# Inverse roots of the norms on GpSimd, and the modulations' products ranked behind 1500 later instructions

## The chip, the cores and the metric

One core of a Trainium2 chip runs the whole program in one launch. The metric is the device time of one execution in microseconds, the median of the runs shown. The engines are TensorE (PE; its weight loads are listed apart as PEld), VectorE (DVE), ScalarE (ACT), GpSimd (POOL) and SyncE (SP), which issues most of the DMAs.

## The reference

A model of 256 tokens with 1024 channels goes through two blocks of two layers each. The first block's layers mix a gated linear recurrence, an mLSTM and a memory attention, then apply a dense feed-forward (layer 0) or a mixture of eight experts (layer 1). The second block is modulated: a condition vector gives each norm a scale and a shift, and each residual a gate.

```python
def rms_norm(x, g):
    xf = x.astype(jnp.float32)
    y = xf * lax.rsqrt(jnp.mean(xf * xf, axis=-1, keepdims=True) + EPS)
    return (y * g.astype(jnp.float32)).astype(x.dtype)
...
def modulate(h, shift, scale):
    return h * (1 + scale) + shift
```

The six modulation vectors of a layer are the condition after a silu, times a 1024 x 6144 matrix, plus a bias. They depend on the conditions alone, so they can be computed at any time before the second block. There are two conditions, that of the tokens and that of a context stream; layer 1 uses the context's first two vectors only.

## The kernel before, in words

**Matmuls in three products.** Every float32 matmul is made of three products of rounded halves: a weight block of 1 MB comes in by a DMA on SP into one of three `raw` tiles (`load`), ACT rounds it to `hi` (L149), DVE subtracts to get `lo` (L150), and PE multiplies hi and lo with the split activations (`proj`, L171 and L175). DVE so has one 128x1024 subtraction to do for every block that PE uses.

**The order of the work.** The program is written as one sequence; a scheduler places each instruction on its engine by rank among those that are ready by its own reckoning, and the rank is the place in the program unless the code shifts it. The result is one fixed list for each engine. An engine runs its list in order: an instruction that has to wait holds up all behind it.

**The mixers.** `mixer` (called for layers 0 and 1 of the first block) first makes the memory attention's queries, scores and weights for four heads (`xa_a`, `xa_b`, `xa_c`). In the last round it adds `gate_rows`, a serial chain of some 20 small DVE steps on 4x256 rows (L399 to L409, a softplus and two scans), whose result PE transposes (L413), and `ml_a`, the first head of the mLSTM: a causal convolution of 8 DVE steps (L344, L347), a silu (L503 on ACT, L504 on DVE) and the split into halves (L368 on ACT, L369 on DVE), which PE needs as the operand of the block products (L171, into `ps_b`). The rest of the mixer is projections with `merge`, `ml_b`, `rg_a` and the like.

**The modulations.** `ada(n)` takes n of a layer's 48 slices. For each it loads 512 KB of the transposed matrix into one of two `adaw` tiles (L1157, on SP) and multiplies it on DVE with the silu of each condition, summing along the row (L1163, one instruction of 128x1024 for each condition with an accumulator). `ada` is called at fixed steps of the mixers (L720, L732, L759) and of the feed-forwards (L839), with the counts of the table `ADA`; `ada_end` does what is left, adds the bias and is followed by the gains. Layer 0's 96 products are made during the first block, layer 1's 64 during the first feed-forward of the second block. `issue_after` binds each product to come behind the last `lo` split that was written before it.

**The norms.** `squares` sums the squares (ACT and DVE, then PE with a column of ones, L251); `rms` scales the sums (L258); `rsqrt` computes an inverse root by a bit trick (L218) and two correction steps, 8 small DVE instructions, each on the result of the one ahead (L218 to L226); `spread` puts the two columns of the result on the diagonals of two 128x128 tiles (L235, DVE) and PE multiplies them with ones (L236), which spreads the roots over all partitions; then DVE multiplies the activations (L272). `rsqrt` is called 21 times: for the norms, and for the heads of the differential attention and of its context part, which do not use `spread`. `spread` runs 12 times, two diagonals each.

Of the kernel before, what the change touches and what calls it, by code (L numbers as in the profile page):

```python
# [8 lines left out]
F32 = mybir.dt.float32  # L9
# [4 lines left out]
OP = mybir.AluOpType  # L14
# [22 lines left out]


ADA = 1, 1, 3, 5


VECS = ["norm_mix_g", "conv_rg_w", "conv_rg_b", "rg_b_a", "rg_b_x", "rg_lambda", "conv_ml_w", "conv_ml_b",
# [67 lines left out]
class Kernel:  # L110
# [102 lines left out]
    def rsqrt(self, v, shape):  # L213


        nc = self.nc
        t = [self.work.tile([128, 8], F32, name=f"rq{i}", bufs=2)[0:shape[0], 0:shape[1]] for i in range(2)]
        nc.vector.tensor_scalar(t[0].bitcast(I32), v.bitcast(I32), -0.5, float(0x5f3759df), op0=OP.mult, op1=OP.add)  # L218
        nc.vector.tensor_mul(t[1], t[0], t[0])
        nc.vector.tensor_mul(t[1], t[1], v)  # L220
        nc.vector.scalar_tensor_tensor(t[1], t[1], -10.0 / 3, t[1], op0=OP.add, op1=OP.mult)

        nc.vector.scalar_tensor_tensor(t[0], t[1], 5.0, t[0], op0=OP.add, op1=OP.mult)
        nc.vector.tensor_mul(t[1], t[0], t[0])
        nc.vector.scalar_tensor_tensor(t[1], t[1], -0.5 * 0.375 ** 3, v, op0=OP.mult, op1=OP.mult)
        nc.vector.scalar_tensor_tensor(t[0], t[1], 1.5 * 0.375, t[0], op0=OP.add, op1=OP.mult)  # L226
        return t[0]

    def spread(self, cols):

        nc = self.nc
        ps = self.bank(self.small)
        for t in range(2):
            dg = self.work.tile([128, 128], F32, name="diag", bufs=2)
            nc.vector.tensor_scalar(dg, self.ident, cols[:, t:t + 1], None, op0=OP.mult)  # L235
            nc.tensor.matmul(ps[:, 0, t * 128:(t + 1) * 128], self.ones[:, :128], dg, start=True, stop=True)  # L236
        return ps

# [456 lines left out]
    def mixer(self, l, raw=None):  # L695
# [15 lines left out]
        for g in range(4):  # L711
# [6 lines left out]
            if g:  # L718
                self.xa_c(X, g - 1, yx)
            self.ada(ADA[2 * l])  # L720
        merged = self.big("merged")
# [3 lines left out]
        for g in range(4):  # L725
# [5 lines left out]
            self.ml_b(M, l, g)  # L731
            self.ada(ADA[2 * l])  # L732
            self.merge(G, l, 2, yx, merged, g)
# [18 lines left out]
        for g in range(4):  # L752
# [5 lines left out]
            if l == 0:  # L758
                self.ada(ADA[0])  # L759
        for j in range(4):  # L760
# [7 lines left out]
    def ffn(self, hs, w1, w3, w2, ff, add, ada=0, between=None, begun=None):  # L768
# [63 lines left out]
        for u in range(n):  # L832
            up(u)
            if u and (one or u < n - 1):
                down([u - 1])
            if begun and u == 0:
                begun()
            else:
                self.ada(ada)  # L839
# [309 lines left out]
    def ada(self, n=1):  # L1149

        nc = self.nc
        for _ in range(n):
            if not self.ada_left:
                break
            l, c = self.ada_left.pop(0)
            raw = self.adap.tile([128, D], F32, name="adaw", bufs=2)
            nc.sync.dma_start(raw, self.A["ada_t"][l, 128 * c:128 * c + 128])  # L1157
            with self.tc.issue_after(self.last_lo.ins):
                for name, s in self.silu.items():
                    if name == "c_ctx_2" and l == 1 and c >= 16:  # L1160
                        continue
                    pr = self.adap.tile([128, D], F32, name="prod", bufs=1)
                    nc.vector.scalar_tensor_tensor(pr, raw, 1.0, s, op0=OP.mult, op1=OP.mult,  # L1163
                                                   accum_out=self.mod[name, l][:, c:c + 1])
# [583 lines left out]
    def second(self):  # L1748
        tc, A = self.tc, self.A
        with ExitStack() as c1:  # L1750
# [8 lines left out]
            with tc.tile_pool(name="adap2", bufs=2) as self.adap:  # L1759
                self.ffn(hs, A["ffn_w1_2"][0], A["ffn_w3_2"][0], A["ffn_w2_2"][0], HID,  # L1760
                         lambda s, j, ps: self.add_mod(s, 0, 1, j, ps), ADA[3], between, lambda: self.ada_layer(1))
            with tc.tile_pool(name="att1", bufs=4) as self.att:
# [75 lines left out]
    def first(self):  # L1838
        tc, A = self.tc, self.A
        with ExitStack() as c1:  # L1840
# [5 lines left out]
            for l in range(2):  # L1846
                self.mixer(l, raw)
                if l == 0:
                    h = self.norm(self.x, self.vec("norm_ffn_g", 0), "h")
                    self.xa_kv(1, 0)  # L1850
                    self.ffn([h], A["ffn_w1"][0], A["ffn_w3"][0], A["ffn_w2"][0], D_FF, self.add_x, ADA[1])
            self.ada_end()
# [38 lines left out]
```

## Time and profile before

| | |
|---|---|
| median of 3 runs | 3192.14 us (3191.67 to 3192.84) |
| the profiled execution | 3190.43 us, its span 3188.6 us |
| mean granted TensorE clock | 0.983 of full speed |
| PE busy | 3094.2 us (97%) |
| DVE busy | 2480.8 us (78%), 3619 instructions |
| ACT busy | 1852.6 us (58%) |
| POOL busy | 70.1 us (2%), 102 instructions |
| HBM | 220 GB/s over the span |

Busy times are averages over stages with different limits: in the first block's mixers and the dense feed-forwards PE has hardly a gap, while in the expert layer (about 1200 to 2160 us) the transfers run at 340 to 350 GB/s and DVE is over 90% busy. A row of the timeline gives start and duration in us, engine, line, operation, tiles, and in brackets the idle time ahead of it with what ended it. "xN" folds N instructions in a row.

### The profile page before, as it was taken

How to read it: one execution, taken by the hardware profiler on the slowest of the kernel's cores; microseconds unless marked ns; L12 is line 12 of the kernel's file. 1: busy time of each engine (PE TensorE's matmuls, PEld its weight loads, DVE VectorE, ACT ScalarE, POOL GpSimd, SP SyncE). 2: the span in 40 equal slices, each digit the busy share in tenths (PEclk: the TensorE clock that was granted, in tenths of full speed). 3: DMA queues.
4: the chain of work that ended last, by engine and by line, in shares of the span. 5: the costliest groups of instructions: out<-in, count | busy, mean ns of one | idle time of the engine just before them, and what ended most of it. 6: DMA issues, size and time to landing. Idle time of an engine off the chain costs nothing. (4 is left out here: it accounts for less than half of the span.)

```text
span 3188.6 us, 53070 instructions
## 1 busy us (share of the span) xinstructions
PE 3094.2 (97%) x21140; PEld 2838.1 (89%) x21140; DVE 2480.8 (78%) x3619; ACT 1852.6 (58%) x2612; POOL 70.1 (2%) x102
## 2 busy tenths in 40 slices
PE   8999999999899999999999999999998999989999
PEld 8899999999899898888888888887988999987999
DVE  7668866678778669999999999997876876676555
ACT  5446644444458457887778878776654222256444
POOL 0000000000000000000000000000320000010000
PEclk9999999999999999999999999999998999999999
DMA  7354656555445559999999999997643444430353
GB/s 273 130 175 159 217 179 219 210 193 213 165 160 180 187 188 345 351 344 348 349 347 335 356 344 341 349 346 241 189 115 128 172 165 166 161 127 31 133 185 119
DMA packets 130873, 712.30 MB, mean 223 GB/s; under 512 B 23352, under 2 KB 35000, under 8 KB 53816
## 3 DMA queue, kind: packets, MB, share of 16 engines
q1 hardware_dynamic: 122552, 701.48, 61.0%
q0 software_dynamic: 8064, 7.34, 1.4%
q8 instruction: 167, 2.74, 0.3%
q14 instruction: 90, 0.74, 0.1%
HBM read 700.38 MB, written 1.05 MB: 220 GB/s over the span
## 5 line engine op out<-in xcount | busy, mean ns | idle before, releaser
L149 ACT CAST hi<-raw 128x1024 fp32r<-128x1024 f32 x1192 | 1233.5, 1051 | 829.7 <-PE ps_a L171 356.6
L150 DVE TENSOR_TENSOR lo<-raw,hi 128x1024 fp32r<-128x1024 f32 x1192 | 1426.5, 1221 | 352.2 <-ACT hi L149 340.0
L171 PE MATMUL ps_a<-hh,hi 128*128 128x256 f32 x2128 | 525.0, 283 | 0.2 <-DVE ks L1261 0.2
L171 PE MATMUL ps_a<-hl,hi 128*128 128x256 f32 x2128 | 524.4, 283 | 0.1
L171 PEld LDWEIGHTS ps_a<-hh,hi 128*128 128x128 f32 x2128 | 401.2, 189 | 4.1 <-issue 2.4
L171 PEld LDWEIGHTS ps_a<-hl,hi 128*128 128x128 f32 x2128 | 401.0, 188 | 3.9 <-issue 3.5
L974 PE MATMUL ps_a<-hi,xsh 128*128 128x512 f32 x896 | 355.0, 396 | 0.0
L975 PE MATMUL ps_a<-hi,xsl 128*128 128x512 f32 x896 | 353.9, 395 | 0.0
L976 PE MATMUL ps_a<-lo,xsh 128*128 128x512 f32 x896 | 351.7, 397 | 0.0
L175 PE MATMUL ps_a<-hh,lo 128*128 128x256 f32 x2128 | 299.3, 282 | 0.0
L175 PEld LDWEIGHTS ps_a<-hh,lo 128*128 128x128 f32 x2128 | 273.8, 188 | 0.5 <-issue 0.4
L825 PE MATMUL ps_b<-gh,lo 128*128 128x256 f32 x752 | 212.3, 283 | 0.0
L824 PE MATMUL ps_b<-gl,hi 128*128 128x256 f32 x752 | 212.1, 283 | 0.0
L823 PE MATMUL ps_b<-gh,hi 128*128 128x256 f32 x752 | 210.5, 283 | 0.0
L975 PEld LDWEIGHTS ps_a<-hi,xsl 128*128 128x128 f32 x896 | 168.3, 188 | 40.0
L976 PEld LDWEIGHTS ps_a<-lo,xsh 128*128 128x128 f32 x896 | 168.3, 188 | 39.5 <-DVE lo L150 0.6
L974 PEld LDWEIGHTS ps_a<-hi,xsh 128*128 128x128 f32 x896 | 168.4, 188 | 37.8 <-issue 0.4
L1006 PE MATMUL ps_b<-hi,mgl 128*128 128x512 f32 x448 | 175.3, 393 | 1.5 <-DVE mgl L992 1.5
L1005 PE MATMUL ps_b<-hi,mgh 128*128 128x512 f32 x448 | 173.8, 391 | 0.0
L825 PEld LDWEIGHTS ps_b<-gh,lo 128*128 128x128 f32 x752 | 144.0, 192 | 0.0
L824 PEld LDWEIGHTS ps_b<-gl,hi 128*128 128x128 f32 x752 | 144.0, 191 | 0.0
L1007 PE MATMUL ps_b<-lo,mgh 128*128 128x512 f32 x448 | 143.8, 396 | 0.0
(564 smaller groups left out, 5675.0 us busy)
## 6 DMA issues: line engine op xcount, KB each, us to landing
raw<-in_moe_w_dram SPq DMA_DIRECT2D x336, 1024.0 KB, 5.9
raw<-in_ffn_w_dram SPq DMA_DIRECT2D x108, 1024.0 KB, 4.8
raw<-in_w_in_dram SPq DMA_DIRECT2D x64, 1024.0 KB, 4.8
adaw<-in_ada_t_dram SPq DMA_DIRECT2D x96, 512.0 KB, 3.8
raw<-in_w_in_ab_dram SPq DMA_DIRECT2D x24, 1024.0 KB, 5.6
raw<-in_w_kv_dram SPq DMA_DIRECT2D x16, 1024.0 KB, 5.0
raw<-in_w_br_xa_dram SPq DMA_DIRECT2D x8, 1024.0 KB, 6.1
raw<-in_w_br_ml_dram SPq DMA_DIRECT2D x8, 1024.0 KB, 4.9
```

The costliest lines, as they stand in the source:

```text
L149: self.last_hi = nc.scalar.copy(hi, view)
L150: self.last_lo = nc.vector.tensor_sub(lo, view, hi.bitcast(F32))
L171: nc.tensor.matmul(out, wh[:, k, :], b[:, k, :], start=start and n == 0, stop=False, skip_group_check=skip)
L175: nc.tensor.matmul(out, wl[:, k, :], xh[:, k, :], start=False, stop=stop and k == nk - 1, skip_group_check=skip)
L823: nc.tensor.matmul(o, wh[:, 0, fs], gh[:, k, :], start=st, stop=False, skip_group_check=True)
L824: nc.tensor.matmul(o, wh[:, 0, fs], gl[:, k, :], start=False, stop=False, skip_group_check=True)
L825: nc.tensor.matmul(o, wl[:, 0, fs], gh[:, k, :], start=False, stop=end, skip_group_check=True)
L974: nc.tensor.matmul(o, xs[0][:, kk, :], wh[:, k, :], start=(kk == 0), stop=False)
L975: nc.tensor.matmul(o, xs[1][:, kk, :], wh[:, k, :], start=False, stop=False)
L976: nc.tensor.matmul(o, xs[0][:, kk, :], wl[:, k, :], start=False, stop=(kk == 7))
L1005: nc.tensor.matmul(o, g[0][:, kk, :], wh[:, 0, ns], start=(c + kk == 0), stop=False)
L1006: nc.tensor.matmul(o, g[1][:, kk, :], wh[:, 0, ns], start=False, stop=False)
```

## The change

All but the first instruction of `rsqrt` move from DVE to GpSimd; there the seven fused steps are written as ten, since each is a plain product or a product or sum with constants, and a third small tile holds one intermediate. The two diagonals of `spread` move to GpSimd as well. The products of `ada` are no longer bound behind the last `lo` split; instead their rank is lowered by 1500 instructions.

```diff
+LATER = 1500
...
     def rsqrt(self, v, shape):
         nc.vector.tensor_scalar(t[0].bitcast(I32), v.bitcast(I32), -0.5, float(0x5f3759df), op0=OP.mult, op1=OP.add)
-        nc.vector.tensor_mul(t[1], t[0], t[0])
-        nc.vector.tensor_mul(t[1], t[1], v)
-        nc.vector.scalar_tensor_tensor(t[1], t[1], -10.0 / 3, t[1], op0=OP.add, op1=OP.mult)
-
-        nc.vector.scalar_tensor_tensor(t[0], t[1], 5.0, t[0], op0=OP.add, op1=OP.mult)
-        nc.vector.tensor_mul(t[1], t[0], t[0])
-        nc.vector.scalar_tensor_tensor(t[1], t[1], -0.5 * 0.375 ** 3, v, op0=OP.mult, op1=OP.mult)
-        nc.vector.scalar_tensor_tensor(t[0], t[1], 1.5 * 0.375, t[0], op0=OP.add, op1=OP.mult)
-        return t[0]
+        pool, (y, w) = nc.gpsimd, t
+        pool.tensor_mul(w, y, y)
+        pool.tensor_mul(w, w, v)
+
+        u = self.work.tile([128, 8], F32, name="rq2", bufs=2)[0:shape[0], 0:shape[1]]
+        pool.tensor_scalar(u, w, -10.0 / 3, None, op0=OP.add)
+        pool.tensor_mul(u, u, w)
+        pool.tensor_scalar(u, u, 5.0, None, op0=OP.add)
+        pool.tensor_mul(y, y, u)
+        pool.tensor_mul(w, y, y)
+        pool.tensor_mul(w, w, v)
+        pool.tensor_scalar(w, w, -0.5 * 0.375 ** 3, 1.5 * 0.375, op0=OP.mult, op1=OP.add)
+        pool.tensor_mul(y, y, w)
+        return y
...
     def spread(self, cols):
-            nc.vector.tensor_scalar(dg, self.ident, cols[:, t:t + 1], None, op0=OP.mult)
+            nc.gpsimd.tensor_scalar(dg, self.ident, cols[:, t:t + 1], None, op0=OP.mult)
...
     def ada(self, n=1):
             nc.sync.dma_start(raw, self.A["ada_t"][l, 128 * c:128 * c + 128])
-            with self.tc.issue_after(self.last_lo.ins):
+
+            with self.tc.high_priority(offset=-LATER):
                 for name, s in self.silu.items():
```

The lists of the engines change with it. Line numbers of the changed kernel are higher: by 1 up to `rsqrt`, by 6 or 7 behind it (L369 is L375 there, L1163 is L1170, L1157 is L1163). Numbers behind a tile's name are those of its copies.

**DVE, mixer of layer 0, from the convolution of the first mLSTM head to its last half.** Before:

```order
L344 TENSOR_SCALAR cv<-pad,vecs 128x256 x2
L494 TENSOR_TENSOR y_xal<-ps_b,y_xah 128x512
L347 SCALAR_TENSOR_TENSOR cv<-pad,vecs,cv 128x256
L150 TENSOR_TENSOR lo<-raw,hi 128x1024
L347 SCALAR_TENSOR_TENSOR cv<-pad,vecs,cv 128x256 x2
L494 TENSOR_TENSOR y_xal<-ps_b,y_xah 128x512
L347 SCALAR_TENSOR_TENSOR cv<-pad,vecs,cv 128x256 x3
L504 SCALAR_TENSOR_TENSOR cv<-th,cv 128x512
L369 TENSOR_TENSOR half<-cv,half 128x512
L369 TENSOR_TENSOR half<-pad,half 128x512
```

With the change:

```order
L353 SCALAR_TENSOR_TENSOR cv<-pad,vecs,cv 128x256 x2
L1170 SCALAR_TENSOR_TENSOR prod,mod_c_570<-adaw,silu_c_574 128x1024
L353 SCALAR_TENSOR_TENSOR cv<-pad,vecs,cv 128x256 x2
L1170 SCALAR_TENSOR_TENSOR prod,mod_c_ctx_572<-adaw,silu_c_ctx_580 128x1024
L500 TENSOR_TENSOR y_xal<-ps_b,y_xah 128x512
L353 SCALAR_TENSOR_TENSOR cv<-pad,vecs,cv 128x256 x2
L1170 SCALAR_TENSOR_TENSOR prod,mod_c_570<-adaw,silu_c_574 128x1024
L510 SCALAR_TENSOR_TENSOR cv<-th,cv 128x512
L1170 SCALAR_TENSOR_TENSOR prod,mod_c_ctx_572<-adaw,silu_c_ctx_580 128x1024
L375 TENSOR_TENSOR half<-cv,half 128x512
L1170 SCALAR_TENSOR_TENSOR prod,mod_c_570<-adaw,silu_c_574 128x1024
L375 TENSOR_TENSOR half<-pad,half 128x512
```

Between these steps stood one `lo` split and no product; now there are five products in the same piece, one ahead of nearly every step. In the whole list up to and with the row of `half<-pad`, there are 10 products before and 61 with the change; the number of `lo` splits is the same. The last of layer 0's 96 products stands at the third `z` (L556 before) of this mixer; before, 16 were made by the end of the mixer's mLSTM part and the rest in the feed-forward and in the mixer of layer 1, where none is left now. Layer 1's 64 products begin at the second block's feed-forward in both.

**PE, the same place, from the attention of the last head to the first block product on `half`.** Before, with the projections (`hh`, `hl`) still between:

```order
L175 MATMUL ps_a<-hh,lo 128x256 x2
L490 MATMUL ps_b<-xpt,xv 128x256 x4
L484 MATMUL ps_b<-consts,xp 128x128 x4
L175 MATMUL ps_a<-hh,lo 128x256 x6
L190 MATMUL ps_a<-y_xah,hi 128x256
L191 MATMUL ps_a<-y_xal,hi 128x256
L490 MATMUL ps_b<-xpt,xv 128x256 x4
L192 MATMUL ps_a<-y_xah,lo 128x256
L171 MATMUL ps_b<-hi,half 128x256
L171 MATMUL ps_b<-lo,half 128x256
```

With the change:

```order
L176 MATMUL ps_a<-hh,lo 128x256 x8
L191 MATMUL ps_a<-y_xah,hi 128x256
L192 MATMUL ps_a<-y_xal,hi 128x256
L193 MATMUL ps_a<-y_xah,lo 128x256
L419 MATMUL ps_b<-consts,r_1188 128x4 x2
L469 MATMUL ps_b<-xk,xq 128x256 x4
L490 MATMUL ps_b<-consts,xp 128x128 x4
L496 MATMUL ps_b<-xpt,xv 128x256 x4
L490 MATMUL ps_b<-consts,xp 128x128 x4
L496 MATMUL ps_b<-xpt,xv 128x256 x4
L172 MATMUL ps_b<-hi,half 128x256
```

Before, the transposes of `gate_rows` (L413, not in this piece) stand well ahead of it and some 50 projections follow them; with the change these projections stand ahead of the transposes, and nothing but the attention is left between the transposes and `half`.

**DVE, the norm of the context stream ahead of the second block's feed-forward (from about 2404 us).** Before:

```order
L223 SCALAR_TENSOR_TENSOR rq_33911<-rq_33912,rq_33911 128x2
L1144 SCALAR_TENSOR_TENSOR silu_c_ctx_34529<-prod,silu_c_ctx_34529 128x1024
L150 TENSOR_TENSOR lo<-raw,hi 128x1024
L247 TENSOR_TENSOR sq<-sq 128x512
L224 TENSOR_TENSOR rq_33912<-rq_33911 128x2
L1223 SCALAR_TENSOR_TENSOR x<-ps_a,mod_c_562,x 128x256 x2
L150 TENSOR_TENSOR lo<-raw,hi 128x1024
L1145 TENSOR_SCALAR silu_c_ctx_34529<-silu_c_ctx_34529 128x1024
L225 SCALAR_TENSOR_TENSOR rq_33912<-rq_33912,ms 128x2
L226 SCALAR_TENSOR_TENSOR rq_33911<-rq_33912,rq_33911 128x2
L1684 TENSOR_SCALAR sinks<-sinks 128x16
L235 TENSOR_SCALAR diag<-consts,rq_33911 128x128 x2
```

With the change:

```order
L151 TENSOR_TENSOR lo<-raw,hi 128x1024
L219 TENSOR_SCALAR rq_33971<-ms 128x2
L151 TENSOR_TENSOR lo<-raw,hi 128x1024
L1150 SCALAR_TENSOR_TENSOR silu_c_34591<-prod,silu_c_34591 128x1024
L151 TENSOR_TENSOR lo<-raw,hi 128x1024
L253 TENSOR_TENSOR sq<-sq 128x512
L1151 TENSOR_SCALAR silu_c_34591<-silu_c_34591 128x1024
L1230 SCALAR_TENSOR_TENSOR x<-ps_a,mod_c_570,x 128x256 x2
L151 TENSOR_TENSOR lo<-raw,hi 128x1024 x2
L1150 SCALAR_TENSOR_TENSOR silu_c_ctx_34597<-prod,silu_c_ctx_34597 128x1024
L151 TENSOR_TENSOR lo<-raw,hi 128x1024
L278 TENSOR_TENSOR xg<-xg,ps_b 128x512 x4
```

The steps of `rsqrt` stood among `lo` splits and the silu of the conditions; only its first one (L219 in the changed kernel) is left in the list, and the product with the spread roots (L278) stands behind five of those splits and three silu steps, with neither roots nor diagonals between. On POOL each `rsqrt` is now a row of ten instructions and each `spread` a pair behind them. SP's list has 12 `adaw` loads in a row ahead of the `raw` load that follows the first mLSTM head's blocks, where one stood.

## Rows read from the trace of the kernel before

**Rows 1.** The page: busy time of the engines, and transfer rates in 40 equal slices.

```profile
PE 3094.2 (97%) x21140; PEld 2838.1 (89%) x21140; DVE 2480.8 (78%) x3619; ACT 1852.6 (58%) x2612; POOL 70.1 (2%) x102
...
GB/s 273 130 175 159 217 179 219 210 193 213 165 160 180 187 188 345 351 344 348 349 347 335 356 344 341 349 346 241 189 115 128 172 165 166 161 127 31 133 185 119
```

**Rows 2.** Windows: PE, PEld, DVE, ACT, POOL busy us (x instructions), PEclk, DMA share, GB/s.

```profile
25.80:151.54 125.74, 120.34 (x954) 116.46 (x954) 90.60 (x148) 58.69 (x95) 0.00 (x0) 0.99 0.50 181
140.00:160.00 20.00, 14.60 (x81) 13.36 (x81) 12.09 (x22) 9.37 (x15) 0.10 (x1) 0.83 0.25 80
160.00:280.00 120.00, 120.00 (x930) 112.07 (x929) 80.60 (x122) 59.89 (x88) 0.41 (x4) 1.00 0.47 163
2440.00:2800.00 360.00, 360.00 (x3019) 359.85 (x3018) 254.64 (x417) 93.94 (x115) 0.00 (x0) 1.00 0.45 159
```

**Rows 3.** Line L1163 and line L1157: the products, and their loads.

```profile
L1163 DVE SCALAR_TENSOR_TENSOR prod<-adaw,silu_c x96: 1210/1219/1228, 46.6 to 2775.9; 128x1024 f32<-128x1024 f32 x96
...
  DMA adaw<-in_ada_t_dram: 10.3, 12
```

```profile
DMA to landing us min/median/max: 3.3/3.8/12.3
```

**Rows 4.** DVE timeline, mixer of layer 0: head 3's scores to the last half.

```profile
134.68 0.69 DVE L467 TENSOR_REDUCE mx<-ps_b 128x2 f32<-128x512 f32 x1 [1.76 <-PE ps_b L463]
...
139.68 1.22 DVE L1163 SCALAR_TENSOR_TENSOR prod<-adaw,silu_c 128x1024 f32<-128x1024 f32 x1
...
140.94 1.22 DVE L1163 SCALAR_TENSOR_TENSOR prod<-adaw,silu_c_ctx 128x1024 f32<-128x1024 f32 x1
...
150.86 0.68 DVE L369 TENSOR_TENSOR half<-pad,half 128x512 fp32r<-128x512 f32 x1
```

**Rows 5.** PE timeline at the same place.

```profile
132.44 0.28 PE L413 MATMUL ps_b<-consts,r 4*128 4x4 f32 x2
...
150.79 0.58 PE L171 MATMUL ps_b<-hi,half 128*128 128x256 f32 x1 [5.40 <-ACT half L368]
151.17 0.42 PE L171 MATMUL ps_b<-lo,half 128*128 128x256 f32 x1
...
157.66 0.40 PE L175 MATMUL ps_b<-half,lo 128*128 128x256 f32 x2
```

**Rows 6.** The same place in the mixer of layer 1: DVE, then PE.

```profile
803.72 0.69 DVE L467 TENSOR_REDUCE mx<-ps_b 128x2 f32<-128x512 f32 x1 [1.76 <-PE ps_b L463]
...
822.43 0.68 DVE L369 TENSOR_TENSOR half<-pad,half 128x512 fp32r<-128x512 f32 x1
```

```profile
822.36 0.58 PE L171 MATMUL ps_b<-hi,half 128*128 128x256 f32 x1 [8.74 <-ACT half L368]
```

**Rows 7.** The context norm ahead of the second block's feed-forward: DVE, then PE.

```profile
2404.64 0.16 DVE L218 TENSOR_SCALAR rq<-ms 128x2 int32<-128x2 int32 x1
...
2418.31 0.16 DVE L226 SCALAR_TENSOR_TENSOR rq<-rq,rq 128x2 f32<-128x2 f32 x1
...
2419.79 0.48 DVE L235 TENSOR_SCALAR diag<-consts,rq 128x128 f32<-128x128 f32 x2
```

```profile
2420.22 0.77 PE L236 MATMUL ps_b<-diag,consts 128*128 128x128 f32 x2 [5.83 <-DVE diag L235]
```

**Rows 8.** Norms for which PE waits, DVE and PE: before the router, before the last feed-forward.

```profile
1098.73 0.16 DVE L218 TENSOR_SCALAR rq<-ms 128x2 int32<-128x2 int32 x1
...
1100.10 0.16 DVE L226 SCALAR_TENSOR_TENSOR rq<-rq,rq 128x2 f32<-128x2 f32 x1
1100.30 0.48 DVE L235 TENSOR_SCALAR diag<-consts,rq 128x128 f32<-128x128 f32 x2
```

```profile
2980.37 1.01 PE L236 MATMUL ps_b<-diag,consts 128*128 128x128 f32 x3 [2.14 <-DVE diag L235]
```

**Rows 9.** POOL by line and shape: busy us, mean ns.

```profile
L1238 POOL TENSOR_TENSOR rt<-rt,late 128x256 f32<-128x256 f32 x18 | 14.5, 803 | 72.7 <-PE ps_a L1236 70.0 <-DVE qc L1253 2.6
...
L1456 POOL TENSOR_TENSOR bias<-bias,late 128x1024 f32<-128x1024 f32 x4 | 9.5, 2373 | 0.3
...
L352 POOL MEMSET pad<- 128x6 f32 x16 | 1.6, 104 | 951.3 <-DVE half L369 781.8 <-DVE cv L347 169.2 <-POOLq L1886 0.3
```

**Rows 10.** The diagonals (L235) on DVE, and one beside POOL's work.

```profile
L235 DVE TENSOR_SCALAR diag<-consts,rq x20: 277/284/1904, 30.5 to 2980.2; 128x128 f32<-128x128 f32 x20
```

```profile
2233.36 1.90 DVE L235 TENSOR_SCALAR diag<-consts,rq 128x128 f32<-128x128 f32 x1
```

```profile
2232.79 2.39 POOL L1456 TENSOR_TENSOR bias<-bias,late 128x1024 f32<-128x1024 f32 x1
```

**Rows 11.** The memory's norm at the start: its diagonals on DVE, their matmuls on PE.

```profile
18.16 0.48 DVE L235 TENSOR_SCALAR diag<-consts,mem_r 128x128 f32<-128x128 f32 x2
```

```profile
21.59 0.61 PE L236 MATMUL ps_b<-diag,consts 128*128 128x128 f32 x4
```

## The prediction, made before the changed kernel ran

> **What bounds the kernel now.** I read the busy times first: PE is busy 97% of the span, DVE 78%, POOL 2% [rows 1]. So the time can fall only where PE waits (3188.6 - 3094.2 = 94 us in all), and it grows wherever PE has to wait longer. Next I read windows of the stages in which the products lie. From 160 to 280 us and from 2440 to 2800 us PE has no gap at all [rows 2]; there DVE work may come and go at no gain, as long as DVE keeps ahead. Then I looked for PE's gaps whose releaser is a DVE or ACT result: 5.40 us ahead of the first block product on `half` in the mixer of layer 0 [rows 5], 8.74 us at the same place of layer 1 [rows 6], 5.83 us ahead of the context norm's spreading [rows 7], and 2 to 4 us at norms with little beside them, such as 2.14 us before the last feed-forward [rows 8]. These four kinds of places are what the change touches.
>
> **The products in the mixer of layer 0.** One product occupies DVE for 1.22 us; two behind each other start 1.26 us apart, and the next instruction follows 1.15 us after [rows 4]; I take 1.15. Nothing makes a product urgent, but the new rank lets it go whenever the scheduler saw DVE free, and a fixed list keeps it there when the chip is late. The list of the changed kernel has 61 products up to the last `half` of the first head, 10 before: 51 more, or 51 x 1.15 = 58.7 us. Seven root steps of 0.16 us and a pair of diagonals of 0.48 us leave DVE in the same piece (durations as in [rows 8]): -1.6 us. From 25.8 us, when the conditions' silu is made, to 151.54 us, the end of that `half` (150.86 + 0.68, [rows 4]), DVE was busy 90.60 of 125.74 us, so idle for 35.1 us [rows 2]. If the products filled every idle moment, `half` would still end 58.7 - 1.6 - 35.1 = **22 us** later, at 173.5 us. That is the low end.
>
> Not every idle moment can be filled. The products need their loads: a pair uses its tile for 2.3 us, the next load lands 3.8 us after its issue [rows 3], and with two tiles a pair can come each (2.3 + 3.8) / 2 = 3.05 us. In the last stretch, from the gate rows on, 15 pairs stand with only short steps between them, which is about 2.7 us a pair by my estimate (2.3 us and two or three steps of 0.16 us); 0.35 us x 15 is some 5 us, of which I take 4. If half of the idle time stayed unfilled, `half` would come 22 + 17.5 = 40 us later: the high end. SP also puts 12 of these loads in a row ahead of a weight block, which then waits for the products that free the tiles. The added traffic itself fits: 26 more loads of 0.52 MB in 125.74 us are 108 GB/s on 181 [rows 2], below the 340 to 350 GB/s that other slices reach [rows 1].
>
> PE cannot hide this. In the changed list the projections that stood between the transposes of the gate rows and `half` lie ahead, so PE does them early, and behind the transposes (132.44 us before, [rows 5]) it has only the attention's few matmuls. It waits for the serial DVE chain, in which a product now stands ahead of almost every step. Afterwards PE is full to 280 us [rows 2], so what is lost is not regained. The half clock after the gap is no new cost: in 140 to 160 us the granted clock averaged 0.83 [rows 2], and the matmuls from 151.17 us on ran about 0.21 us apart until 157 us [rows 5]; a longer gap has the same end. Of the products left after `half` there are 35 instead of 6; 29 x 1.15 = 33 us fit in the 39.4 us that DVE idles in 160 to 280 us [rows 2], and PE is later too. I put **+26 us** (20 to 40) for this stage.
>
> **The mixer of layer 1 and the feed-forward** lose 80 products. In full stretches that is worth nothing. At the gap of 8.74 us, scores to last `half` took 822.43 + 0.68 - 803.72 = 19.4 us with six products between, in layer 0 150.86 + 0.68 - 134.68 = 16.9 us with two [rows 4, 6]: 0.63 us a product. Six gone give **-4 us** (0 to -8.7, the whole gap).
>
> **The context norm at 2404 us.** DVE takes 13.8 us from the first root step to the last, because splits stand between them, and PE waits 5.83 us [rows 7]. On POOL the steps stand alone (below, about 4 us with the diagonals), so the diagonals are done before PE asks. But the token stream's update now stands behind the norm's products in DVE's list, and PE then waits for the split activations. I take **-4 us** (0 to -10).
>
> **The price of a root on POOL.** No POOL instruction in the trace has a 128x2 shape. A memset of 128x6 takes 0.10 us, a two-input product of 128x256 takes 0.80 us, one of 128x1024 2.37 us [rows 9]. The line through the last two, (2.37 - 0.80) / 768 = 2.05 ns an element, leaves 0.28 us at no elements; I take that, step for step. Ten steps are 2.8 us (1.0 by the memset, 8.0 by the 128x256 product), against 1.53 us on DVE undisturbed (1098.73 to 1100.26, [rows 8]); the diagonals of 128 elements are 0.28 + 0.26 = 0.54 us each against 0.28 us. An exposed norm so becomes 1.4 us longer by the roots and 0.5 us by the diagonals. Three are fully exposed (before the router, before the last feed-forward, at the end), +5.7 us; four in the differential attention, the router's own root and the entry to the second block are partly so, and I take +2.3 us for them together. Sum **+8 us** (-2 by the low price, +30 by the high one). Norms with full PE work beside them cost nothing; the cover is the projections of the stage before.
>
> Here a rule speaks against the change. What the trace shows first: the memory's diagonals start at 18.16 us and their matmuls at 21.59 us [rows 11], so this first root has 2.9 us to spare and I cost it at nothing. The Trainium skill, page GPSIMD Engine Reference, section Instruction dispatch, says that the first call of freshly loaded code costs about 6 us that no row of a profile shows; by that rule the first root on POOL would overrun its slack by some 3 us and the sum below would be 3 us higher. No row of this trace shows it.
>
> **The sum.** 26 - 4 - 4 + 8 = +26 us on the profiled execution's 3190.4 us is 3216 us; the runs' median lies 1.7 us above that execution, so **3218 us**, 0.8% slower.
>
> **Rivals.**
> *The idle time swallows the products (faster).* In layer 1 an added product cost 0.63 us of the chain, not 1.15, since the chain waits for ACT and PE anyway. If that holds for the 51 of layer 0, they need 32 us, less than the 35.1 us of idle time, and `half` is not later. It decides at 35.1 / 51 = 0.69 us a product. Then nothing is lost there, and -6 in layer 1, -6 at the context norm and +2 at the norms give -10 us: 3182 us. For it: DVE idles 28% of that stretch. Against it: the layer 1 figure comes from six products in a chain full of waits, while in layer 0 some 30 of the 51 stand among splits, ahead of the gate rows, where DVE waits for little but ACT.
> *The gains and losses cancel.* A third of the 26 us stays (+9), layer 1 gives -6, the norm -6, the roots +3: 3192 us. It needs the same as the rival above, half true.
> *POOL is dear.* Each small step costs what the 128x256 product does, 0.8 us, and DVE is held meanwhile. For it: a diagonal that DVE began at 2233.36 us, while POOL worked from 2232.79 us on a bias tile, took 1.90 us where the median is 0.284 us [rows 10]. Then the norms cost +30 to +50 instead of +8, and the time is about 3255 us. Against it: the steps move two elements a partition, and the slow diagonal stood beside an instruction of 1024. The Trainium skill, page Advanced Engine Details and Errata, section VectorE Performance Modes, says that the second SBUF port of VectorE is shared with GpSimd and that the two block each other; the slow diagonal agrees (1.90 us against 0.284 us), and the rule would lengthen DVE work beside each root.
>
> **How the numbers follow.** The forecast gets 0.72, POOL dear 0.08, cancelling 0.10, faster 0.10. The forecast's own range is 3204 to 3240 (mixer 20 to 40, norms 0 to 12, the gaps -2 to -14). Down to the cancelling case and a little below it, 3190, and up to 3242, about 0.8 is held. A difference of 0.2%, 6.4 us, is about what can be told from no change: faster 0.10, same 0.10, slower 0.80.
>
> **What would show it.** In the mixer of layer 0, PE's gap ahead of the first block product on `half` grows from 5.4 us to 25 us or more, split between the gate rows' transposes, the scores and `half`, and that `half` ends at 173 us or later; no product lies in layer 1's chain and its gap is 4 to 5 us; the context norm's gap is below 2 us; ten POOL steps take about 2.8 us; the gap before the last feed-forward is about 4 us. I am wrong if `half` of layer 0 ends before 160 us, if POOL's steps take over 0.5 us each, or if PE gets new gaps between 160 and 280 us for late `lo` splits.

## The result, and the profile after

The changed kernel takes 3215.52 us (median of 4 runs, 3213.01 to 3217.53) against 3191.9 us for the kernel before beside it: a ratio of 1.0074 [1.0057, 1.0092], so 0.74% slower. The forecast was 3218 us. The total is right, and not all of its terms are: the products of layer 1, the roots with their norms and the mixer of layer 0 cost more than forecast, and a gain of about 18 us that the forecast did not know of paid for them.

The profiled execution took 3217.53 us (span 3215.8 us, mean granted TensorE clock 0.977). The busy line of its page answers to [rows 1]: DVE lost 27 us of work to POOL, which gained 102 us, and PE's busy time fell by 6 us while the span grew by 27.

```profile
PE 3088.1 (96%) x21140; PEld 2828.6 (88%) x21140; DVE 2454.0 (76%) x3448; ACT 1852.6 (58%) x2612; POOL 172.4 (5%) x336
```

**Mixer of layer 0.** Windows of the changed kernel (columns as in [rows 2]), the first of them from the silu of the conditions to the end of the first head's last `half`:

```profile
25.80:181.97 156.17, 126.78 (x957) 120.71 (x956) 144.10 (x242) 58.55 (x95) 9.06 (x12) 0.91 0.65 228
...
140.00:160.00 20.00, 7.27 (x31) 5.57 (x29) 18.52 (x36) 1.47 (x2) 0.00 (x0) 0.66 0.48 167
160.00:180.00 20.00, 6.26 (x21) 4.76 (x22) 18.97 (x39) 6.78 (x16) 0.00 (x0) 0.74 0.43 146
```

DVE is now busy 18.5 to 19.0 of 20 us around the gate rows and the attention, where it was busy 12.1 of 20 [rows 2], and PE only 6 to 7. The timeline of PE shows what it waited for, in the order of the serial chain (answers to [rows 5]):

```profile
145.16 0.39 PE L193 MATMUL ps_a<-y_xah,lo 128*128 128x256 f32 x1 [2.85 <-DVE lo L151]
...
154.90 0.37 PE L419 MATMUL ps_b<-consts,r 4*128 4x4 f32 x2 [9.36 <-DVE r L411]
...
162.96 3.58 PE L496 MATMUL ps_b<-xpt,xv 128*128 128x256 f32 x8 [3.28 <-ACT xpt L492]
...
179.75 0.58 PE L172 MATMUL ps_b<-hi,half 128*128 128x256 f32 x1 [10.06 <-ACT half L374]
```

On DVE one product stands ahead of each of the last two splits (answers to [rows 4]); the last one ends at 181.28 + 0.69 = 181.97 us, 30.4 us later than before:

```profile
178.39 1.22 DVE L1170 SCALAR_TENSOR_TENSOR prod<-adaw,silu_c_ctx 128x1024 f32<-128x1024 f32 x1
...
179.54 0.69 DVE L375 TENSOR_TENSOR half<-cv,half 128x512 fp32r<-128x512 f32 x1
180.14 1.23 DVE L1170 SCALAR_TENSOR_TENSOR prod<-adaw,silu_c 128x1024 f32<-128x1024 f32 x1
...
181.28 0.69 DVE L375 TENSOR_TENSOR half<-pad,half 128x512 fp32r<-128x512 f32 x1
```

**Mixer of layer 1.** Without products the gap of 8.74 us [rows 6] is 4.97 us:

```profile
837.25 0.58 PE L172 MATMUL ps_b<-hi,half 128*128 128x256 f32 x1 [4.97 <-ACT half L374]
```

**Norms.** A root on POOL where DVE does nothing beside it, ahead of the last feed-forward (POOL's timeline; the first and the last of ten steps, then the diagonals), and PE behind it, answering to [rows 8]:

```profile
3004.71 0.20 POOL L221 TENSOR_TENSOR rq<-rq 128x2 f32<-128x2 f32 x1 [60.57 <-DVE rq L219]
...
3007.28 0.20 POOL L232 TENSOR_TENSOR rq<-rq,rq 128x2 f32<-128x2 f32 x1
3007.57 1.19 POOL L241 TENSOR_SCALAR diag<-consts,rq 128x128 f32<-128x128 f32 x2
```

```profile
1114.95 1.38 PE L242 MATMUL ps_b<-diag,consts 128*128 128x128 f32 x4 [5.67 <-POOL diag L241]
...
2430.06 0.79 PE L242 MATMUL ps_b<-diag,consts 128*128 128x128 f32 x2 [2.90 <-POOL diag L241]
...
3008.24 1.38 PE L242 MATMUL ps_b<-diag,consts 128*128 128x128 f32 x4 [4.01 <-POOL diag L241]
```

Ten steps take 2.85 us from 3004.71 to 3007.57 us, a step 0.20 us with a start each 0.28 us, a diagonal 0.60 us. The gap before the last feed-forward grew from 2.14 to 4.01 us, that of the context norm (2430.06 us) shrank from 5.83 [rows 7] to 2.90 us.

### The profile page after: what moved, and what is told of

Read it like the earlier page. It is cut to its first block, busy times and chain, and to the rows that moved or that the text cites. A ratio compares the mean times of both kernels' runs of the same rounds, so it can differ in the third digit from the quotient of the medians.

```text
span 3215.8 us, 53166 instructions
## 1 busy us (share of the span) xinstructions
PE 3088.1 (96%) x21140; PEld 2828.6 (88%) x21140; DVE 2454.0 (76%) x3448; ACT 1852.6 (58%) x2612; POOL 172.4 (5%) x336
## 5 line engine op out<-in xcount | busy, mean ns | idle before, releaser
L829 PEld LDWEIGHTS ps_b<-gh,hi 128*128 128x128 f32 x752 | 142.9, 191 | 1.0 <-DVE ctx L1230 1.0
```

The lines of the kernel that those rows point to most:

```text
L829: nc.tensor.matmul(o, wh[:, 0, fs], gh[:, k, :], start=st, stop=False, skip_group_check=True)
```

## The experiments

**The two kernels again.** For a second trace of each on one chip; nothing edited.

> The kernel before, unchanged, for a second profile. In the last feed-forward (3000 to 3170 us), where the change moves nothing, PE's matmuls of 128x256 started 119.95 ns apart in the first profile of before and 118.3 ns apart in that of the change. If that pace belongs to the single execution or the chip, this profile shows any value near 118 to 120 ns, most likely that of its neighbours in this job; if it belongs to the kernel, it shows 119.9 ns again. Time 3190 to 3193 us either way.

> The changed kernel, unchanged, for a second profile on the same chip as the others of this job. 3213 to 3218 us. Pace of the matmuls in the last feed-forward 118.3 ns if the pace belongs to the kernel, that of the kernel before on this chip if it belongs to the execution. PE's gap ahead of the first block product on half in layer 0 and the waits just ahead of it add to 25 us again.

Measured: 3187.66 and 3216.74 us. Places agree: the block product on `half` starts at 180.16 us in the second trace of the change. PE's waits ahead of it add up to 22.6 us there and to 26.3 us in the first trace, where 25 us were expected.

**Each half alone.** `pool_only` has the roots and diagonals on GpSimd, the products bound behind the last `lo` as before; `ada_only` has the ranked products, roots and diagonals on DVE:

```diff
-            with self.tc.issue_after(self.last_lo.ins):
+            with self.tc.high_priority(offset=-LATER):
```

> The roots and diagonals on GpSimd as in the change, the products of the modulations bound behind the last split as before. My theory (the products in layer 0's mixer make the loss): 3192 to 3200 us, +8 for roots that PE waits for and -4 at the context norm. Rival (POOL is dear): 3212 us or more. PE waits for diagonals 2 us longer before the router and before the last feed-forward under either.

> The products ranked behind the next 1500 instructions as in the change, roots and diagonals on VectorE as before. My theory: 3205 to 3222 us, nearly the whole loss, with PE's waits between the gate rows' transposes and half in layer 0 at 20 us or more. Rival (POOL is dear): 3188 to 3195 us. Its list has 66 products up to that half, the change's 61.

Measured: `pool_only` 3184.63 us, 0.9974 [0.9965, 0.9983], faster than before. `ada_only` 3237.42 us, 1.0142 [1.0126, 1.0157]. So the products are the loss, and more than all of it. But a gain by roots on POOL contradicts the longer gaps shown above. The new matter in its trace was that matmuls came closer together in stretches where PE never waits. The third small tile of a root, in two copies 64 bytes in each of the 128 partitions, moves every tile that is allocated after it; by the program's allocation (the traces show no addresses) the first activation tile lies 96 bytes behind a multiple of 512 before and 160 with the change.

**Only the place of the tiles.** `spare64` and `spare416` are the kernel before with a tile that nothing uses, so that all that is allocated later moves by 64 or by 416 bytes (to a multiple of 512); the instructions and their order stay the same, on every engine of the traces. `pool_in_place` is `pool_only` with the third operand in spare columns of the second tile, so that nothing moves. `ranked_spare64` is `ada_only` moved by 64 bytes.

```diff
+            self.work.tile([128, 16], F32, name="spare", bufs=1)
```

```diff
-        u = self.work.tile([128, 8], F32, name="rq2", bufs=2)[0:shape[0], 0:shape[1]]
+        u = wide[0:shape[0], 4:4 + shape[1]]
```

> The kernel before with one tile of 64 bytes a partition that nothing uses, reserved where the third small tile of the changed rsqrt lies; every engine's list of instructions stays the same, and the activations' tiles move up by 64 bytes, as in the change. Theory A (PE's pace follows the tiles' place in SBUF): matmuls of 128x256 in the last feed-forward 118.3 ns apart instead of 119.95, time 3174 to 3183 us. Theory B (the pace comes from the work on POOL or from the other order): 119.95 ns and 3189 to 3195 us.

> The same with 416 bytes, which puts the first block's activation tiles on a multiple of 512 bytes. Theory A: a pace of 118.3 ns or less, time 3165 to 3183 us, the lower the more the place matters. Theory B: 119.95 ns and 3189 to 3195 us.

> Roots and diagonals on GpSimd, products bound as before, with the third operand in the free half of the second tile, so that no other tile moves; lists as in the run with the roots alone. Theory A: pace 119.95 ns, and the time is that of the roots' own price, 3195 to 3206 us (my +4, or more by the waits seen: +1.9 before the router, +1.9 before the last feed-forward, +5 at the context norm of the last mixer). Theory B: 118.3 ns and 3182 to 3187 us.

> The products ranked as in the change, roots on VectorE, plus the unused 64 bytes. Theory A: 3219 to 3228 us, the 3237 of the run without the spare bytes less what they are worth. Theory B: 3235 to 3240 us. Under A the rest, against the change's 3215.5, is what roots on GpSimd are worth when the products crowd VectorE.

Measured, against 3190.53 us: `spare64` 3172.86 us, 0.9941 [0.9927, 0.9955]; `spare416` 3191.32 us, 1.0002 [0.9993, 1.0011]; `pool_in_place` 3201.18 us, 1.0035 [1.0021, 1.0049]; `ranked_spare64` 3220.8 us, 1.0096 [1.008, 1.0111]. One window of 80 us inside the last feed-forward shows it in each. First `before_again`, then `spare64`, `spare416`, `pool_in_place` and the changed kernel:

```profile
3060.00:3140.00 80.00, 80.00 (x669) 80.00 (x668) 41.98 (x42) 34.58 (x38) 0.00 (x0) 1.00 0.53 184
```

```profile
3060.00:3140.00 80.00, 80.00 (x679) 80.00 (x678) 43.19 (x43) 34.46 (x37) 0.00 (x0) 1.00 0.51 182
```

```profile
3060.00:3140.00 80.00, 80.00 (x669) 80.00 (x668) 41.77 (x42) 34.43 (x37) 0.00 (x0) 1.00 0.52 185
```

```profile
3060.00:3140.00 80.00, 80.00 (x670) 80.00 (x669) 42.12 (x41) 34.73 (x38) 0.00 (x0) 1.00 0.52 185
```

```profile
3060.00:3140.00 80.00, 80.00 (x680) 80.00 (x679) 42.77 (x43) 35.44 (x38) 0.00 (x0) 1.00 0.52 185
```

PE is busy for all of the 80 us at the full clock in every one, and gets 669 or 670 matmuls done, or 679 or 680: 1.5% more, with the tiles 64 bytes further on. Moving the tiles to a multiple of 512, for which a gain was expected as well, changed nothing. The place is worth 3172.86 - 3190.53 = -17.7 us here, and two more pairs of runs that differ by it alone say the same: `pool_only` against `pool_in_place` -18.4 us, `ranked_spare64` against `ada_only` -14.8 us, each run set against the kernel before beside it. So the change contains this gain by accident, and the roots on GpSimd by themselves cost 3201.18 - 3190.53 = +10.7 us. With the products ranked as well the same edit gains: the change is 5.3 us below `ranked_spare64`, presumably since the steps then leave a DVE list in which products stand ahead of them.

**One layer's products at a time.** The changed kernel, with one layer's products bound as before (`layer0_ranked` shown; `layer1_ranked` has `l == 0`):

```diff
-            with self.tc.high_priority(offset=-LATER):
+            with (self.tc.issue_after(self.last_lo.ins) if l == 1 else self.tc.high_priority(offset=-LATER)):
```

> The changed kernel with the lowered rank for layer 0's products alone; layer 1's products are bound behind the last split, as before. The run with roots on GpSimd and all products bound took 3184.6 us. Theory (two separate losses, about +24 by the end of the first block and +11 in the second): 3205 to 3212 us. Rival, that of the prediction (only the mixer of layer 0 loses): 3213 to 3217 us, the change's own time.

> The same with the lowered rank for layer 1's 64 products alone. Theory (two losses): 3192 to 3199 us, all of it between the context norm at about 2400 us and the second block's first feed-forward. Rival of the prediction (products in the second block are free): 3182 to 3187 us.

Measured: `layer0_ranked` 3209.76 us, 1.0053 [1.004, 1.0067]; `layer1_ranked` 3191.72 us (3184.5 to 3199.03 in 11 runs), 0.9997 [0.9988, 1.0006]. Against `pool_only` that is +25.1 us for layer 0, of which the mixers give +29 and -4, and +7.1 us for layer 1, which the forecast had at nothing. These are differences of runs on two chips, on which the kernel before took 3193.81 and 3192.33 us; with each run set against the kernel before on its own chip, they are +23.7 and +5.6 us. PE's block product on `half` starts at 179.31 us in `layer0_ranked` and at 149.96 us in `layer1_ranked`. First `layer0_ranked`, then `layer1_ranked`:

```profile
179.31 0.58 PE L172 MATMUL ps_b<-hi,half 128*128 128x256 f32 x1 [7.51 <-ACT half L374]
```

```profile
149.96 0.58 PE L172 MATMUL ps_b<-hi,half 128*128 128x256 f32 x1 [5.34 <-ACT half L374]
```

Where layer 1's products cost time shows in POOL's timeline at the token stream's norm ahead of the second block's feed-forward. In the changed kernel, with products on DVE beside it:

```profile
2446.05 1.15 POOL L221 TENSOR_TENSOR rq<-rq 128x2 f32<-128x2 f32 x1 [15.45 <-DVE rq L219]
2447.27 0.20 POOL L222 TENSOR_TENSOR rq<-rq,ms 128x2 f32<-128x2 f32 x1
...
2448.15 1.30 POOL L227 TENSOR_SCALAR rq<-rq 128x2 f32<-128x2 f32 x1
...
2453.96 1.94 POOL L241 TENSOR_SCALAR diag<-consts,rq 128x128 f32<-128x128 f32 x2
```

The same steps in `pool_only`, where DVE waits in this stretch:

```profile
2416.85 0.19 POOL L221 TENSOR_TENSOR rq<-rq 128x2 f32<-128x2 f32 x1 [10.51 <-DVE rq L219]
...
2419.70 1.20 POOL L241 TENSOR_SCALAR diag<-consts,rq 128x128 f32<-128x128 f32 x2
```

And DVE in the changed kernel, over the first of these steps and over those of 2448 us:

```profile
2445.91 1.22 DVE L1170 SCALAR_TENSOR_TENSOR prod<-adaw,silu_c_ctx 128x1024 f32<-128x1024 f32 x1
...
2448.16 1.23 DVE L1170 SCALAR_TENSOR_TENSOR prod<-adaw,silu_c 128x1024 f32<-128x1024 f32 x1 [1.01 <-DMA adaw<-in_ada_t_dram]
...
2456.55 2.48 DVE L278 TENSOR_TENSOR xg<-xg,ps_b 128x512 f32<-128x512 f32 x4 [1.11 <-PE ps_b L242]
```

First step to first diagonal takes 7.91 us (2446.05 to 2453.96) against 2.85 us: a POOL step that meets a product takes 1.15 to 1.30 us, one that runs while DVE waits for the next load (2447.3 to 2448.1) 0.20 us. From PE's spreading of the context norm to DVE's use of the token norm it is 2456.55 - 2430.06 = 26.5 us, against 2423.21 - 2405.81 = 17.4 us in `pool_only`. Of these 9.1 us, 4.95 lie ahead of the first step, where three products stand in DVE's list (2437.86, 2443.39 and 2444.65 us), and 5.06 between the first step and the first diagonal; from there on it is 0.9 us less. PE has fill work at this place, so that its gaps stay below 2.1 us, but it does less: windows of 2440 to 2480 us, first the changed kernel, then `pool_only`.

```profile
2440.00:2480.00 40.00, 36.26 (x243) 35.30 (x244) 35.31 (x65) 12.63 (x24) 9.00 (x12) 0.79 0.43 143
```

```profile
2440.00:2480.00 40.00, 40.00 (x340) 40.00 (x339) 34.84 (x56) 12.45 (x15) 0.00 (x0) 1.00 0.49 172
```

The two windows are not the same work (the change is 24 us later at 2430), so their counts are no price. Counted matmul by matmul, PE's list is 24.2 us behind that of `pool_only` when it comes to the spreading of the context norm, and 36.0 us behind from 2471 us on: 11.8 us in these two traces, against +7.1 us in the medians of the runs. Longer gaps are only some 3.4 us of it. The rest is the clock: behind its gaps PE runs at 0.50 of the full clock from 2440 to 2445 and from 2460 to 2465 us, the lower of its two levels, while in `pool_only` it is at 1.00 from 2426 us on. A smaller part can come further on, where a product that waits for its load holds DVE: in the trace of `layer1_ranked`, the slowest of its 11 runs, one waits 4.74 us for `adaw` at 2539.24 us, PE waits 2.64 us at 2587.85 us for a DVE result (L1230), and its list falls back by 4.3 us more; in the changed kernel's trace it is 1 us there.

**Two versions.** `tuned_a` is the kernel before with the activation tiles and the pair tiles both moved to 160 bytes behind a multiple of 512, and the second entry of `ADA` 2 instead of 1. `tuned_b` is `tuned_a` with the root and diagonals of one norm, the context norm ahead of the second block's feed-forward, on GpSimd in place.

```diff
+            self.pairp.tile([128, 40], F32, name="spare0", bufs=1)
...
+            self.work.tile([128, 104], F32, name="spare1", bufs=1)
```

> The kernel before with two unused tiles (160 and 416 bytes) that put the activations' tiles and the pair tiles at 160 modulo 512 bytes, and the counts of the modulations at 1, 2, 3, 5 instead of 1, 1, 3, 5, so that the dense feed-forward takes the products that stood in layer 1's mixer. By the pace of the matmuls on pair tiles (120 ns to about 117.5) and the gap of 8.7 us in layer 1 shrinking to 5: 3158 to 3166 us. If the place matters for the activation tiles alone: 3167 to 3171 us. If products in the dense feed-forward cost as much as in the mixer: 3172 us or more.

> The same, and the root and diagonals of the one context norm ahead of the second block's feed-forward on GpSimd, in place (no third tile). Where the roots on GpSimd stood in place, PE was 4.6 us earlier behind that norm: 3 to 5 us less than the run with the tiles and counts alone. Rival (the norm's gain goes into the next wait, the split of the activations): no difference within 1.5 us.

Measured: `tuned_a` 3172.11 us, 0.9933 [0.9919, 0.9946], no better than `spare64`, where 3158 to 3166 was expected. The 128x256 matmuls on pair tiles came down from 120 to 118 ns, but the 128x512 ones on pair tiles in the expert layer (`mgh`, `mgl`) went from about 228.5 to 233 ns: the stage takes 1113.4 us, 1106.7 in `spare64`, which gives back what the fewer products in layer 1's mixer and the pair tiles gained. `tuned_b` takes 3165.67 us, 0.9917 [0.9903, 0.9931], the fastest here. Its PE waits 2.88 us at the context norm; in `tuned_a` it is 6.07 us. The 6.4 us between the two are not all shown to be the norm's: over this norm PE's list gains 2.6 us in the traces, and the pace of the matmuls differs as well (last section).

## Why the prediction was right in its total, point by point

| term | forecast | measured | from |
|---|---|---|---|
| products of layer 0, mixer 0 | +26 | +29 | start of the block product on `half`, both traces |
| products of layer 0, mixer 1 | -4 | -3.8 | gap of 8.74 and 4.97 us |
| products of layer 1, second block | 0 | +7.1 | `layer1_ranked` to `pool_only` |
| roots and context norm | +8 - 4 | +10.7 | `pool_in_place` to before |
| place of the tiles | none | -17.7 | `spare64` to before |
| sum | +26 | +25.3 | change to before: +23.6 |

The terms follow one path: first the roots on GpSimd, then the place, then the products. In another order they differ, since roots and products share DVE: on one place the products cost 3220.8 - 3172.86 = 47.9 us with the roots on DVE, and 30.9 us (3215.52 - 3184.63) with them on GpSimd.

**Mixer of layer 0: right, slightly low.** The mechanism held: DVE ran out of idle time, and each product ahead of a serial step pushed it back. DVE was idle for 156.17 - 144.10 = 12.1 us up to the end of `half` where I left 4 us, of which 5.1 us were waits for `adaw`; and it had 144.1 - 90.6 = 53.5 us of added work, not 57.1. 53.5 - 35.1 + 12.1 = 30.5 us is the delay of `half`. The waits for the loads over the whole program grew from 10.3 us in 12 cases [rows 3] to these (line L1163, who waited for it):

```profile
  DVE prod L1170: 32.3, 25
```

I had expected at least 25 us in PE's gap ahead of the first block product, split in three parts; it is 9.36 + 3.28 + 10.06 = 22.7 us, plus 2.85 us at a late `lo`. PE is then full again up to 310 us except for 1.1 us, so what was lost stayed lost; the sign of being wrong, new gaps for late `lo` splits, came to 0.49 us. The half clock behind the gap was no new cost, as forecast: PE is back at the full clock by 185 us, 5 us behind the start on `half`; before, it was back between 155 and 160 us, 4 to 9 us behind it.

**Mixer of layer 1: right.** 8.74 to 4.97 us, by the 0.63 us that a product cost of this chain.

**Products in the second block: wrong, and this step failed.** I read from [rows 2] that PE has no gap from 2440 to 2800 us and took DVE work there to be free. The products rank by place in the program, and the freed ones went to the head of the stage, among the two norms ahead of the full stretch; they cost 5.6 to 7.1 us by the runs. A window that begins where PE is already fed says nothing of the chain that feeds it.

**Roots on GpSimd: the price of a step right, the sum too low by 7 us.** The estimates were 2.8 us for ten steps (2.85 measured) and 0.54 us for a diagonal (0.60). The exposed norms became 1.9 us longer each, as forecast: 2.14 to 4.01, and 3.79 to 5.67 us at 1114.95 us. (The forecast's own figures make it 1.8: the roots' share is 2.8 - 1.53 = 1.27 us, not 1.4.) Two things were missed. I did not list the context norm of the last mixer (about 2816 us), and I priced a norm by its gap alone. PE's waits for this norm's split activations are three in `before_again`, 1.82 + 1.47 + 0.41 = 3.7 us, and two in `pool_in_place`, 4.32 + 3.23 = 7.6 us:

```profile
2812.49 0.38 PE L190 MATMUL ps_a<-h_ctxh,hi 128*128 128x256 f32 x1 [1.82 <-ACT h_ctxh L280]
```

```profile
2815.78 0.58 PE L191 MATMUL ps_a<-h_ctxh,hi 128*128 128x256 f32 x1 [4.32 <-ACT h_ctxh L287]
...
2819.81 0.58 PE L192 MATMUL ps_a<-h_ctxl,hi 128*128 128x256 f32 x1 [3.23 <-DVE h_ctxl L288]
```

Behind them PE is busy in both, at the full clock in the one and at 0.75 in the other, and does 87 matmuls in 10 us against 67:

```profile
2820.00:2830.00 10.00, 10.00 (x87) 10.00 (x87) 8.02 (x23) 6.67 (x16) 0.00 (x0) 1.00 0.22 91
```

```profile
2820.00:2830.00 10.00, 10.00 (x67) 10.00 (x68) 3.46 (x10) 2.51 (x6) 1.62 (x8) 0.75 0.33 126
```

And a root is only as fast as 2.85 us if DVE stands still. The context norm's steps beside four `lo` splits and the silu take 8.87 us (2420.53 to 2429.40), so its gap closed to 2.9 us and not to nothing. In `pool_in_place` PE reaches this norm only 0.9 us later than in `before_again`, having been 5.5 us behind at 2215 us, and is 11 us behind at 2872 us. Its list keeps at 0.8 us behind from 2450 to 2790 us, so that nearly all of these 10 us arise in the last mixer, at its context norm and behind it: waits that are 3.9 us longer, gaps of 2.7 us at 2836 to 2839 us that `before_again` does not have, and the lower clock. That norm is the step of this term that failed; it was not run by itself.

**"POOL is dear" was half true.** The rival said that each small step would take 0.8 us and that DVE would be held. A step beside two-input work of DVE does take 1.0 to 1.3 us, yet the DVE instruction keeps its length: the products of the rows above take 1.22 and 1.23 us, as in [rows 4]. Here GpSimd is the one that waits. It can go the other way: the slow diagonal of [rows 10] ended at 2235.26 us on DVE, just behind POOL's instruction at 2235.18 us. The Trainium skill, page Advanced Engine Details and Errata, section VectorE Performance Modes, says that VectorE's second SBUF port is shared with GpSimd, so that GpSimd instructions and VectorE instructions that use both ports block each other; the trace agrees for POOL (0.20 to 1.2 us) and shows no loss on DVE in these rows. The Trainium skill, page GPSIMD Engine Reference, section Instruction dispatch, says that the first call of freshly loaded code costs about 6 us; nothing of that size shows here: the first root on POOL runs from 15.29 to 18.88 us with steps of 0.19 to 0.73 us, and the memory's matmuls follow without a gap.

**The rivals that were faster or equal did not come.** The 51 products were not absorbed by DVE's idle time; the kernel with all of the change but the gain of the place would be about 18 us slower than it is.

**The place of the tiles was no step at all.** I counted the third tile as no cost. That the total came out right is luck: this -17.7 us stood against +7 for layer 1's products, +7 for the roots and norms and +3 for the mixer.

## What to carry to other kernels

Work that "nothing waits for" is free only where the engine's list has slack over the whole way to the next serial chain: ranked freely it moves into that chain, one instruction ahead of each of its steps. Small steps moved to GpSimd take what they take alone only while no VectorE instruction holds them up, so look at what stands beside them. A wait of PE is priced by its length and by the matmuls behind it at the lower clock. Before an edit that adds a tile is judged, run the old kernel with an unused tile of the same size.

## What was not expected of the hardware

PE's pace, at the full granted clock and without a wait, changes with where in the partition the operand tiles lie: 669 matmuls of 128x256 in 80 us with the first activation tile 96 bytes behind a multiple of 512 or on it, 679 at 160 bytes. In `spare64` it is the matmuls on the activation tiles `hh` and `hl` that come closer together, from 119.9 to 117.8 ns over the program; some 6800 of them make 14 us. Those on pair tiles in the same feed-forwards (`gh`, `gl`) stay at 119.8 ns until `tuned_a` moves their tiles, and the 512-wide ones on `mgh` and `mgl` then go the other way.

The place is not the whole account. `tuned_a` and `tuned_b` place the tiles alike, and differ in pace all the same: 685 and 676 matmuls in the window of the last feed-forward (first `tuned_a`, then `tuned_b`), but 676 and 684 in 540 to 620 us.

```profile
3060.00:3140.00 80.00, 80.00 (x685) 80.00 (x684) 42.80 (x43) 35.01 (x38) 0.00 (x0) 1.00 0.49 179
```

```profile
3060.00:3140.00 80.00, 80.00 (x676) 80.00 (x676) 42.20 (x42) 35.42 (x38) 0.00 (x0) 1.00 0.47 171
```

Why the place matters, and what else does, is open: only these three places of the activation tiles were run, and the place of the weights was not varied by itself.
